# A two-block fp32 network on one core: modulation rows spread over three stages, a two-half norm on VectorE, and recurrence products grouped by the rows they use

## Chip, cores and metric

The kernel runs on one core of a Trainium2 chip. The metric is the device time of one execution in microseconds (us); lower is better. The five engines go by the names of the profile: PE (TensorE matmul, with PEld its weight load), DVE (VectorE), ACT (ScalarE), POOL (GpSimd) and SP (SyncE, which issues the DMAs).

## The reference, cut to what matters

All values are float32, the model width D is 1024. `first_block` maps 256 tokens; `second_block` runs two layers over these tokens and, in its first layer, over 256 context tokens too.

```python
def first_block(x, ...):
    x = x + 0.5 * swiglu(rms_norm(x, ffn1_norm), ffn1_w_in, ffn1_w_out)
    h = rms_norm(x, mix_norm)
    p_rwkv, p_q, p_k, p_v, p_gate = split(h @ w_in)
    y_a = rwkv7_time_mix(p_rwkv, ...)           # recurrence over 256 tokens, 16 heads
    y_b = dilated_attention(p_q, p_k, p_v, ...)
    g_a, g_b = split(sigmoid(p_gate + b_gate))
    x = x + (g_a * (y_a @ w_proj_rwkv) + g_b * (y_b @ w_proj_attn)) @ w_out
    return x + 0.5 * swiglu(rms_norm(x, ffn2_norm), ffn2_w_in, ffn2_w_out)

def rms_norm(x, g):
    return x * rsqrt(mean(x * x, axis=-1) + 1e-6) * g

def step(state, inp):                            # inside rwkv7_time_mix
    sa = einsum('bhvk,bhk->bhv', state, a_t)
    state = state * w_t + sa * b_t + v_t * k_t
    return state, einsum('bhvk,bhk->bhv', state, r_t)
```

In the second block each layer has six modulation rows of 1024 columns per stream, a product of one conditioning vector with `w_ada_2` (1024 by 6144). They scale and shift the norms and gate the residuals: shift, scale and gate of the mixer (columns 0 to 3D), then shift, scale and gate of the ffn (3D to 6D). A mixer runs three branches one after the other, `mlstm`, `diffattn` and `fourier`, each followed by gates and a projection.

## The kernel before

**Matrix products.** Every large product is done in three parts, high times high, low times high and high times low, so each block of weights is needed twice over. `weights` streams them: a 512 KB DMA brings a block `wr` (4 buffers), ACT casts it to `wh` (L202), DVE subtracts to get `wl` (L203), with 3 buffers of each, and PE multiplies (L214 to L216 with tokens on the output rows, L249 to L251 with tokens on the columns). One pass of the loop in `weights` is called a weight iteration here. A scheduler that keeps the data dependences orders the instructions of each engine; on each engine they then run strictly in that order.

**Modulation rows.** `ada(l, c0, c1)` computes columns c0 to c1 in blocks of 512. A block has 8 steps; a step loads 256 KB of `w_ada_2` (`wa`, 4 buffers) and runs two DVE operations, one for each stream, that add a scaled weight block into `aa` (L1134). Then `finish` sums `aa` over the rows with two products on PE (`ada`, L1119; four passes in the trace), copies them on ACT and writes them to memory. `ada` is a generator in `self.fine`; each weight iteration advances it by `self.rate` steps, and what is left when the ffn's own loop is through is run off in one go. The first block's two ffns have 66 weight iterations each, so at rate 0.4 each takes 26 of 48 steps (six blocks, 3D columns) in its loop and, as the code is written, 22 behind it. Layer 1's rows run in layer 0's ffn at rate 1.5.

**Norms.** `rms_row` squares and sums 1024 columns on ACT (L330) and takes the inverse root on POOL: nine small operations on one column, each waiting for the one before it (L331, L286, L290, and L292 and L293 three times). `norm_steps` multiplies x by its gain on DVE (L338) and, when POOL is through, by the root in two halves (L344, or L346 with a shift); PE then transposes the halves (`tr`, L317). There are 22 such norms, two of them the final one, which multiplies at L1602 and L1604 and writes a 1024-column row block with one DMA. `outgoing` runs an output product in two column halves and hands the token tile to the norm when both have been added to X (L459 or L462 and L463).

**The recurrence.** `rwkv_solve` runs for two halves of the heads, eight heads each. In each half it goes over four chunks of 64 tokens. A chunk has, for each head, a product over 128 rows (L818) and, from the second chunk on, a product over 64 rows with the state S (L820), both added up in the same 64 columns of a PSUM tile `pf`. There are two such tiles, one for each parity of the head number; the heads of one parity keep their state in the lower 64 rows, those of the other in the upper 64. ACT copies the outputs O (L824), DVE scales the new state S (L830). Each product shows as two passes in the trace.

## Time and profile before

| what | value |
|---|---|
| median of 3 runs | 2996.85 us (2996.62 to 3001.39) |
| profiled execution, its own time | 3002.16 us |
| its span, first to last instruction | 3000.4 us |
| mean granted TensorE clock | 0.963 of full speed |
| PE / DVE / ACT / POOL busy | 96% / 63% / 40% / 4% |

The span and every row below belong to the one profiled execution. A busy PE is not a PE at its best: its matmuls are pipelined, they run at the clock that was granted at the time (full speed, or half of it), and a switch between kinds of products counts as busy. So a PE that is 96% busy can still lose time in three ways: by idling, at the lower clock, or with products that take longer than they need.

### The profile page before, as it was taken

How to read it: one execution, taken by the hardware profiler on the slowest of the kernel's cores; microseconds unless marked ns; L12 is line 12 of the kernel's file. 1: busy time of each engine (PE TensorE's matmuls, PEld its weight loads, DVE VectorE, ACT ScalarE, POOL GpSimd, SP SyncE). 2: the span in 40 equal slices, each digit the busy share in tenths (PEclk: the TensorE clock that was granted, in tenths of full speed). 3: DMA queues.
4: the chain of work that ended last, by engine and by line, in shares of the span. 5: the costliest groups of instructions: out<-in, count | busy, mean ns of one | idle time of the engine just before them, and what ended most of it. 6: DMA issues, size and time to landing. Idle time of an engine off the chain costs nothing.

```text
span 3000.4 us, 42489 instructions
## 1 busy us (share of the span) xinstructions
PE 2866.2 (96%) x16536; PEld 2436.1 (81%) x16536; DVE 1895.7 (63%) x3228; ACT 1186.0 (40%) x1955; POOL 123.9 (4%) x278
## 2 busy tenths in 40 slices
PE   8988899988998999999999999999999999999998
PEld 7976787777996888987788977877778897799797
DVE  7776958576767455436674266677664555665655
ACT  4434334234443344225442333222344444444443
POOL 1020000002002000000000001000020000000000
PEclk9999979679999999999999999999999999999999
DMA  8766535055674222231233355554442243255564
GB/s 266 222 200 205 169 97 147 32 180 186 211 222 130 67 67 64 75 103 50 64 124 99 88 165 150 159 173 151 155 134 85 85 139 102 78 152 169 168 188 142
DMA packets 298356, 409.59 MB, mean 137 GB/s; under 512 B 31525, under 2 KB 182949, under 8 KB 298154
## 3 DMA queue, kind: packets, MB, share of 16 engines
q1 hardware_dynamic: 298154, 406.87, 44.5%
q8 instruction: 130, 2.13, 0.3%
q14 instruction: 72, 0.59, 0.1%
HBM read 396.98 MB, written 3.24 MB: 133 GB/s over the span
## 4 chain that ended last, share of the span: by engine, by line
PE 80%; DVE 10%; issue 3%; ACT 3%; POOL 2%; DMA 1%; SPq 0%; ACTq 0%; POOLq 0%; DVEq 0%
PE g L215 11%; PE g L216 11%; PE g L214 11%; PE g L249 11%; PE g L251 10%; PE g L250 10%; DVE wl L203 2%; PE dC L1342 2%; PE tr L317 1%; PE I L1318 1%; DVE aa L1134 1%; PE pf L818 1%; ACT dae L1439 1%; PE pf L820 1%; PE f L1509 1%
## 5 line engine op out<-in xcount | busy, mean ns | idle before, releaser
L203 DVE TENSOR_TENSOR wl<-wr,wh 128x1024 fp32r<-128x1024 f32 (+1 forms) x606 | 733.5, 1212 | 630.7 <-ACT wh L202 628.8
L202 ACT CAST wh<-wr 128x1024 fp32r<-128x1024 f32 (+1 forms) x606 | 631.2, 1042 | 1056.2 <-PE g L216 515.6
L215 PE MATMUL g<-wl,xh 128*128 128x512 f32 (+2 forms) x1880 | 733.2, 390 | 13.0 <-DVE wl L203 13.0
L214 PE MATMUL g<-wh,xh 128*128 128x512 f32 (+2 forms) x1880 | 730.0, 391 | 4.4 <-ACT wh L202 2.1
L216 PE MATMUL g<-wh,xl 128*128 128x512 f32 (+2 forms) x1880 | 728.3, 388 | 0.1
L249 PE MATMUL g<-xh,wh 128*128 128x256 f32 (+1 forms) x2352 | 725.9, 309 | 2.2 <-DVE gate L981 1.5
L251 PE MATMUL g<-xh,wl 128*128 128x256 f32 (+1 forms) x2352 | 723.2, 308 | 2.3 <-DVE wl L203 2.3
L250 PE MATMUL g<-xl,wh 128*128 128x256 f32 (+1 forms) x2352 | 722.3, 307 | 0.0
L249 PEld LDWEIGHTS g<-xh,wh 128*128 128x128 f32 x2352 | 452.9, 193 | 33.2 <-issue 7.0
L251 PEld LDWEIGHTS g<-xh,wl 128*128 128x128 f32 x2352 | 453.0, 193 | 25.8 <-DVE wl L203 2.9
L250 PEld LDWEIGHTS g<-xl,wh 128*128 128x128 f32 x2352 | 452.8, 193 | 20.7 <-issue 1.3
L215 PEld LDWEIGHTS g<-wl,xh 128*128 128x128 f32 x1880 | 359.3, 191 | 88.0 <-DVE wl L203 19.5
L214 PEld LDWEIGHTS g<-wh,xh 128*128 128x128 f32 x1880 | 356.6, 190 | 84.1 <-issue 7.5
L216 PEld LDWEIGHTS g<-wh,xl 128*128 128x128 f32 x1880 | 359.4, 191 | 70.5 <-DVE xl L305 1.5
L1134 DVE SCALAR_TENSOR_TENSOR aa<-wa,cond,aa 128x512 f32<-128x512 f32 x336 | 231.9, 745 | 4.8 <-DMA wa<-in_w_ada_dram 4.7
L304 ACT CAST xh<-tr 128x256 fp32r<-128x256 f32 (+1 forms) x114 | 50.4, 463 | 119.8 <-PE tr L317 107.0
L1439 ACT ACTIVATE dae<-sc,dast 128x512 f32<-128x512 f32 (+1 forms) x96 | 58.5, 614 | 42.2 <-DVE dast L1437 37.3
L305 DVE TENSOR_TENSOR xl<-tr,xh 128x256 fp32r<-128x256 f32 (+1 forms) x114 | 57.4, 531 | 18.8 <-ACT xh L304 18.4
L1437 DVE TENSOR_REDUCE dast<-sc 128x1 f32<-128x512 f32 (+1 forms) x96 | 53.8, 597 | 24.2 <-PE sc L1436 23.8
L317 PE MATMUL tr<-ident,hn 128*128 128x128 f32 x160 | 28.5, 315 | 34.1 <-DVE hn L344 17.6
L317 PEld LDWEIGHTS tr<-ident,hn 128*128 128x128 f32 x160 | 22.1, 163 | 43.1 <-DVE hn L344 18.4
L1119 PE MATMUL ada<-aa,one 128*1 128x512 f32 x96 | 30.6, 646 | 27.7 <-DVE aa L1134 27.6
(386 smaller groups left out, 2693.9 us busy)
## 6 DMA issues: line engine op xcount, KB each, us to landing
wr<-in_w_in_dram SPq DMA_DIRECT2D x156, 512.0 KB
wa<-in_w_ada_dram SPq DMA_DIRECT2D x192, 256.0 KB
wr<-in_ffn_w_in_dram SPq DMA_DIRECT2D x88, 512.0 KB
wr<-in_w_ffn_in_dram SPq DMA_DIRECT2D x84, 512.0 KB
wr<-in_w_in_dram SPq DMA_DIRECT2D x156, 256.0 KB
wr<-in_w_ffn_out_dram SPq DMA_DIRECT2D x50, 512.0 KB
wr<-in_ffn_w_out_dram SPq DMA_DIRECT2D x44, 512.0 KB
wr<-in_w_out_dram SPq DMA_DIRECT2D x32, 512.0 KB
```

The costliest lines, as they stand in the source:

```text
L202: nc.scalar.copy(out=wh[:, :kn, :ntot], in_=src)
L203: nc.vector.tensor_tensor(out=wl[:, :kn, :ntot], in0=src, in1=wh[:, :kn, :ntot].bitcast(F32), op=ALU.subtract)
L214: nc.tensor.matmul(o_, xh, wh[:, n0:n1], start=(kc == 0), stop=False)
L215: nc.tensor.matmul(o_, xh, wl[:, n0:n1], start=False, stop=False)
L216: nc.tensor.matmul(o_, xl, wh[:, n0:n1], start=False, stop=(kc == nk - 1))
L249: nc.tensor.matmul(o_, wh[:, fs], xh, start=(kc == 0), stop=False)
L250: nc.tensor.matmul(o_, wh[:, fs], xl, start=False, stop=False)
L251: nc.tensor.matmul(o_, wl[:, fs], xh, start=False, stop=(kc == nk - 1))
L317: self.nc.tensor.transpose(p[:, j * P:(j + 1) * P], src[:, (c + j) * P:(c + j + 1) * P], self.ident)
L1134: nc.vector.scalar_tensor_tensor(out=y, in0=raw, scalar=self.cond[:, k, s:s + 1], in1=acc[s], op0=ALU.mult, op1=ALU.add)
L1342: nc.tensor.matmul(pc[:, 0:257], kw[:, kc * P:(kc + 1) * P], V[t][:, 0:257], start=True, stop=True)
L1439: nc.scalar.activation(out=em, in_=ps[:, 0:n], func=AF.Exp, bias=st[:, m:m + 1], scale=1.0, accum_out=st[:, 2 + m:3 + m])
```

## The change

It has three parts.

- **Modulation rows.** ffn1 now takes columns 0 to 2D (four blocks, 32 steps) at rate 0.6, ffn2 takes 2D to 4D at the same rate, and layer 0's `fourier` branch with its gates takes 4D to 6D at rate 1.4. What is left is run off behind the gates. The gates of the other two branches move into the inner memory pool's scope.
- **Norms.** The sum of squares is split: ACT does columns 0 to 511 as soon as `outgoing` has added them to X (`first_half`), DVE does columns 512 to 1023 with a multiply that accumulates. The inverse root moves from POOL to DVE with a start value that folds in the factor of one half: one operation joins the halves, then come seven more of one column. The final norm multiplies x, root and gain in one operation per half, and each half has a DMA of its own.
- **The recurrence.** A chunk's eight products over 128 rows come first, for both parities into two banks; the eight over 64 rows with the state follow, alternating between lower and upper rows. Copies and states come after them.

```diff
+    def first_half(self, t, x):
+        nc = self.nc
+        a = self.sums[t] = self.s(1, "rn_a", bufs=4)
+        nc.scalar.activation(out=self.h([P, 512], F32, "junk"), in_=x[:, 0:512], func=AF.Square, accum_out=a)
+        nc.vector.tensor_scalar(out=a, in0=a, scalar1=-0.5 / D, scalar2=-0.5e-6, op0=ALU.mult, op1=ALU.add)
+
+    def rms(self, t, x, junk):
...
+        a = self.sums.pop(t)
+        h, y, w = self.s(1, "rn_h"), self.s(1, "rn_y"), self.s(1, "rn_w")
+        nc.vector.scalar_tensor_tensor(out=junk, in0=x[:, 512:D], scalar=1.0, in1=x[:, 512:D], op0=ALU.mult,
+                                       op1=ALU.mult, accum_out=h)
+        nc.vector.tensor_scalar(out=h, in0=h, scalar1=-0.5 / D, scalar2=a[:, 0:1], op0=ALU.mult, op1=ALU.add)
+
+        nc.vector.tensor_scalar(out=y.bitcast(I32), in0=h.bitcast(I32), scalar1=-0.5,
+                                scalar2=float(0x5F3759DF - 0x400000 - 0x40000000), op0=ALU.mult, op1=ALU.add)
+        for _ in range(3):
+            nc.vector.tensor_scalar(out=w, in0=y, scalar1=y[:, 0:1], scalar2=h[:, 0:1], op0=ALU.mult, op1=ALU.mult)
+            nc.vector.tensor_scalar(out=y, in0=w, scalar1=1.5, scalar2=y[:, 0:1], op0=ALU.add, op1=ALU.mult)
+        return y
...
+                banks = [self.t("pf") for _ in range(2)]
+                at = lambda par, pair: banks[par][:, pair * 64:(pair + 1) * 64]
+                for par in range(2):
+                    for pair in range(4):
+                        h = pair * 2 + par
+                        nc.tensor.matmul(at(par, pair), GBf[:, eidx(h), c, 64:192], WV[t][:, c, h, :], start=(pair == 0),
+                                         stop=(ch == 0 and pair == 3))
+                if ch:
+                    for pair in range(4):
+                        for par in range(2):
+                            rows = slice(64 * par, 64 * par + 64)
+                            nc.tensor.matmul(at(par, pair), RG[rows, pair, c].rearrange("p s k -> p (s k)"),
+                                             S[rows, pair, :], start=False, stop=(pair == 3))
...
-            self.fine, self.rate = self.ada(0, 0, 3 * D), 0.4
+            self.fine, self.rate = self.ada(0, 0, 2 * D), 0.6
...
-            self.fine, self.rate = self.ada(0, 3 * D, 6 * D), 0.4
+            self.fine, self.rate = self.ada(0, 2 * D, 4 * D), 0.6
...
+                with self.inner() as self.ip:
+                    if need_ctx:
+                        self.fine, self.rate = self.ada(0, 4 * D, 6 * D), 1.4
+                    self.fourier(xT, W, outs, yT)
+                    gates = {c0: gate(c0) for c0 in range(0, D, n)}
+                    for _ in self.fine:
+                        pass
```

**Place 1: PE at the end of ffn1.** The `g` rows are products (of 512 columns in ffn1, of 288 in the projection behind it), `tr` the norm's transposes, `ada` the products of a modulation block. Before:

```order
L215 MATMUL g<-wl,xh 128x512
L216 MATMUL g<-wh,xl 128x512
L1119 MATMUL ada<-aa,one 1x512 x8
L317 MATMUL tr<-ident,hn 128x128 x12
L214 MATMUL g<-wh,xh 128x288
```

And now:

```order
L215 MATMUL g<-wl,xh 128x512
L216 MATMUL g<-wh,xl 128x512
L309 MATMUL tr<-ident,hn 128x128 x8
L214 MATMUL g<-wh,xh 128x288
L215 MATMUL g<-wl,xh 128x288
L216 MATMUL g<-wh,xl 128x288
```

The eight products of four modulation blocks have left this place, and the first tile's transposes stand directly behind the last product of ffn1; the second tile's eight come 18 products later.

**Place 2: DVE at the same place.** X_69 and X_70 are the two token tiles, `hn` the normed tile, `rn_*` the one-column values of the root, `aa` the modulation sums. Before:

```order
L459 SCALAR_TENSOR_TENSOR X_69<-g,X_69 128x512
L338 TENSOR_TENSOR hn<-X_69,gain 128x1024
L203 TENSOR_TENSOR wl<-wr,wh 128x2x288
L344 TENSOR_SCALAR hn<-hn,rn_y 128x512 x2
L203 TENSOR_TENSOR wl<-wr,wh 128x2x288
L459 SCALAR_TENSOR_TENSOR X_70<-g,X_70 128x512
L1134 SCALAR_TENSOR_TENSOR aa<-wa,cond,ab 128x512
L338 TENSOR_TENSOR hn<-X_70,gain 128x1024
L1134 SCALAR_TENSOR_TENSOR aa<-wa,cond,ab 128x512
L1134 SCALAR_TENSOR_TENSOR aa<-wa,cond,aa 128x512 x14
```

And now:

```order
L481 SCALAR_TENSOR_TENSOR X_69<-g,X_69 128x512
L332 SCALAR_TENSOR_TENSOR hn,rn_h<-X_69 128x512
L334 TENSOR_SCALAR rn_h<-rn_h,rn_a 128x1
L336 TENSOR_SCALAR rn_y<-rn_h 128x1
L339 TENSOR_SCALAR rn_w<-rn_y,rn_h 128x1
L203 TENSOR_TENSOR wl<-wr,wh 128x2x288
L340 TENSOR_SCALAR rn_y<-rn_w,rn_y 128x1
L339 TENSOR_SCALAR rn_w<-rn_y,rn_h 128x1
L340 TENSOR_SCALAR rn_y<-rn_w,rn_y 128x1
L203 TENSOR_TENSOR wl<-wr,wh 128x2x288
```

The modulation sums (32 operations in all behind ffn1) are gone from here; the root's small operations now stand in DVE's row, with the `wl` of the next weights between them.

**Place 3: PE in a recurrence chunk of the first half of the heads.** `pf` with its number is one of the two PSUM tiles, WV and GB belong to the products over 128 rows, S and RG to those over 64 rows. Before, the end of one tile and the start of the other:

```order
L818 MATMUL pf_4023<-WV_2731,GB_2729 128x64
L820 MATMUL pf_4023<-S_3703,RG_3927 128x64
L818 MATMUL pf_4033<-WV_2731,GB_2729 128x64
L820 MATMUL pf_4033<-S_3703,RG_3927 128x64
L818 MATMUL pf_4033<-WV_2731,GB_2729 128x64
```

And now:

```order
L839 MATMUL pf_3933<-WV_2641,GB_2639 128x64 x4
L839 MATMUL pf_3934<-WV_2641,GB_2639 128x64 x4
L845 MATMUL pf_3933<-S_3613,RG_3837 128x64
L845 MATMUL pf_3934<-S_3613,RG_3837 128x64
L845 MATMUL pf_3933<-S_3613,RG_3837 128x64
```

Each row of L818 was followed by one of L820; now the eight over 128 rows stand together, and the eight over 64 rows go to the two tiles in turn.

## Rows read from the trace of the kernel before

**Rows 1.** The page: engines' busy time, and the chain that ended last by engine

```profile
PE 2866.2 (96%) x16536; PEld 2436.1 (81%) x16536; DVE 1895.7 (63%) x3228; ACT 1186.0 (40%) x1955; POOL 123.9 (4%) x278
...
PE 80%; DVE 10%; issue 3%; ACT 3%; POOL 2%; DMA 1%; SPq 0%; ACTq 0%; POOLq 0%; DVEq 0%
```

**Rows 2.** Waits of the span: engine and line, releaser, total us, times, longest us

```profile
PE ada L1119 <- DVE aa L1134: 27.6, 3, 13.2
...
PE tr L317 <- DVE hn L344: 17.6, 3, 11.9
...
PE tr L317 <- DVE hn L346: 16.5, 7, 6.0
...
ACT O L824 <- PE pf L820: 50.7, 12, 5.6
```

**Rows 3.** TensorE's timeline, end of ffn1: start us, us, work, passes, [idle before <-releaser]

```profile
207.53 1.88 PE L1119 MATMUL ada<-aa,one 128*1 128x512 f32 x8
...
222.66 2.53 PE L1119 MATMUL ada<-aa,one 128*1 128x512 f32 x4 [13.25 <-DVE aa L1134]
...
233.66 2.53 PE L1119 MATMUL ada<-aa,one 128*1 128x512 f32 x4 [8.47 <-DVE aa L1134]
...
236.12 1.91 PE L317 MATMUL tr<-ident,hn 128*128 128x128 f32 x12
```

**Rows 4.** VectorE's timeline, same stretch

```profile
203.56 0.69 DVE L459 SCALAR_TENSOR_TENSOR X<-g,X 128x512 f32<-128x512 f32 x1 [1.77 <-PE g L216]
...
213.91 9.36 DVE L1134 SCALAR_TENSOR_TENSOR aa<-wa,cond,aa 128x512 f32<-128x512 f32 x14
```

**Rows 5.** Windows: us, busy PE, PEld, DVE, ACT, POOL (xinstructions), granted clock, DMA share, GB/s

```profile
40.00:200.00 160.00, 160.00 (x1110) 147.78 (x1109) 126.52 (x154) 71.78 (x81) 2.13 (x5) 1.00 0.76 233
330.00:650.00 320.00, 290.26 (x1929) 240.40 (x1930) 226.16 (x537) 111.91 (x237) 3.60 (x7) 0.79 0.39 116
540.00:551.00 11.00, 11.00 (x42) 8.47 (x43) 1.58 (x4) 1.75 (x7) 0.00 (x0) 0.50 0.00 0
1600.00:1750.00 150.00, 150.00 (x904) 133.69 (x903) 48.80 (x64) 47.38 (x65) 0.00 (x0) 1.00 0.30 89
```

**Rows 6.** TensorE's timeline, end of ffn2

```profile
917.24 2.52 PE L1119 MATMUL ada<-aa,one 128*1 128x512 f32 x4 [5.93 <-DVE aa L1134]
...
926.80 0.80 PE L215 MATMUL g<-wl,xh 128*128 128x512 f32 x1 [2.55 <-DVE wl L203]
```

**Rows 7.** Timeline of all engines, the norm at the end of layer 1's mixer

```profile
2787.05 0.69 DVE L463 TENSOR_TENSOR X<-X,rs 128x512 f32<-128x512 f32 x1
...
2793.27 0.75 DVE L346 SCALAR_TENSOR_TENSOR hn<-hn,rn_y,mod 128x512 f32<-128x512 f32 x1 [2.54 <-POOL rn_y L293]
...
2794.08 1.12 PE L317 MATMUL tr<-ident,hn 128*128 128x128 f32 x4 [5.98 <-DVE hn L346]
```

**Rows 8.** VectorE's timeline: two dependent operations of one column

```profile
2275.51 0.16 DVE L1325 SCALAR_TENSOR_TENSOR mlrc<-nd 128x1 f32<-128x1 f32 x1
...
2275.71 0.16 DVE L1327 TENSOR_TENSOR mlrc<-mlrc,mlcf 128x1 f32<-128x1 f32 x1
```

**Rows 9.** TensorE's timeline, recurrence products of several chunks

```profile
392.36 0.43 PE L818 MATMUL pf<-WV,GB 128*128 128x64 f32 x2
...
392.72 0.44 PE L820 MATMUL pf<-S,RG 64*128 64x64 f32 x4
...
530.25 2.10 PE L818 MATMUL pf<-WV,GB 128*128 128x64 f32 x16
...
540.71 0.69 PE L818 MATMUL pf<-WV,GB 128*128 128x64 f32 x2
...
550.58 0.69 PE L768 MATMUL p<-WV,GB 64*64 64x64 f32 x8
```

**Rows 10.** Timeline, the end: last product, last write of y

```profile
2986.85 0.39 PE L216 MATMUL g<-wh,xl 128*128 128x512 f32 x1
...
2996.07 0.76 DVE L1604 TENSOR_SCALAR y<-y,fin_y 128x1024 f32<-128x1024 f32 x1 [3.21 <-POOL fin_y L293]
```

More of the change, by code (lines that the diff above doesn't have):

```diff
@@ L282, in rsqrt @@
         nc = self.nc
[L283 removed]
         y = self.s(n, name + "_y")
         w = self.s(n, name + "_w")
[L286 removed]
+        nc.vector.tensor_scalar(out=y.bitcast(I32), in0=m.bitcast(I32), scalar1=-0.5, scalar2=float(0x5F3759DF),
                                 op0=ALU.mult, op1=ALU.add)
[L288 to L294 removed]
         for _ in range(3):
@@ L324, in to_split @@
                 d += m
-    def rms_row(self, x, name="rn"):
+    def first_half(self, t, x):
         nc = self.nc
-        junk = self.q([P, D], F32, "junk")
-        ss = self.s(1, name + "_s")
-        nc.scalar.activation(out=junk, in_=x, func=AF.Square, accum_out=ss)
-        nc.gpsimd.tensor_scalar(out=ss, in0=ss, scalar1=1.0 / D, scalar2=1e-6, op0=ALU.mult, op1=ALU.add)
-        return self.rsqrt(ss, 1, name)
+        a = self.sums[t] = self.s(1, "rn_a", bufs=4)
[3 more added lines that the diff above has]
+        nc = self.nc
+        if t not in self.sums:
+            self.first_half(t, x)
+        a = self.sums.pop(t)
[9 more added lines that the diff above has]
+        return y
     def norm_steps(self, xT, t, x, gain, shift):
@@ L337, in norm_steps @@
         hn = self.q([P, D], F32, "hn")
-        nc.vector.tensor_tensor(out=hn, in0=x, in1=gain, op=ALU.mult)
-        r = self.rms_row(x)
+        half = lambda v, c: v[:, c:c + 512]
+        if shift is not None:
+            nc.vector.tensor_tensor(out=half(hn, 0), in0=half(x, 0), in1=half(gain, 0), op=ALU.mult)
+        r = self.rms(t, x, half(hn, 512))
+        if shift is not None:
+            nc.vector.tensor_tensor(out=half(hn, 512), in0=half(x, 512), in1=half(gain, 512), op=ALU.mult)
         yield
         for c in range(0, D, 512):
-            v = hn[:, c:c + 512]
+            v = half(hn, c)
             if shift is None:
-                nc.vector.tensor_scalar(out=v, in0=v, scalar1=r[:, 0:1], scalar2=None, op0=ALU.mult)
+                nc.vector.scalar_tensor_tensor(out=v, in0=half(x, c), scalar=r[:, 0:1], in1=half(gain, c), op0=ALU.mult,
+                                               op1=ALU.mult)
             else:
-                nc.vector.scalar_tensor_tensor(out=v, in0=v, scalar=r[:, 0:1], in1=shift[:, c:c + 512], op0=ALU.mult,
+                nc.vector.scalar_tensor_tensor(out=v, in0=v, scalar=r[:, 0:1], in1=half(shift, c), op0=ALU.mult,
                                                op1=ALU.add)
@@ L431, in normed, with outgoing, begin @@
         return xT, done
-    def outgoing(self, xT, nk, W, groups, res, done):
+    def outgoing(self, X, xT, nk, W, groups, res, done):
         whole = lambda g: [(t, 0, 512) for t in g]
+        def begin(g):
+            for t in g:
+                self.first_half(t, X[t])
         if len(groups[0]) > 1:
@@ L440, in outgoing @@
                     res(g, c, self.gemm(xT, nk, W[c], whole(g)))
+                    if c == 0:
+                        begin(g)
                 done(g)
@@ L992, in last_projection @@
                 self.put_split(mT.dst_span(i * per, per, 0, w), M[i].rearrange("p (k t) -> p k t", t=w))
-        self.outgoing(mT, KD, [[(w_out, 0, c * 512, 512)] for c in range(2)], groups, res, nxt())
+        self.outgoing(X, mT, KD, [[(w_out, 0, c * 512, 512)] for c in range(2)], groups, res, nxt())
     def first_block(self, X, nxt):
@@ L1539, in second_layer @@
             yT = SplitT(self, KD, w)
+            gate = lambda c0: [g for c in range(c0, c0 + n, 256) for g in self.gate_chunk(xT, W, U_GATE + b * D + c, w)]
             if fn == "fourier":
-                self.fourier(xT, W, outs, yT)
+                with self.inner() as self.ip:
[5 more added lines that the diff above has]
+                        pass
             else:
@@ L1545, in second_layer @@
                     getattr(self, fn)(xT, W, l, outs, yT)
-            gate = lambda c0: [g for c in range(c0, c0 + n, 256) for g in self.gate_chunk(xT, W, U_GATE + b * D + c, w)]
-            gates = {c0: gate(c0) for c0 in range(0, D, n)}
+                gates = {c0: gate(c0) for c0 in range(0, D, n)}
             if b < 2:
@@ L1601, in done @@
                     y = self.q([P, D], F32, "y")
-                    nc.vector.tensor_tensor(out=y, in0=X[t], in1=g, op=ALU.mult)
-                    r = self.rms_row(X[t], "fin")
-                    nc.vector.tensor_scalar(out=y, in0=y, scalar1=r[:, 0:1], scalar2=None, op0=ALU.mult)
-                    nc.sync.dma_start(out=out[0, t * P:(t + 1) * P, :], in_=y)
+                    r = self.rms(t, X[t], y[:, 512:D])
+                    for c in range(0, D, 512):
+                        nc.vector.scalar_tensor_tensor(out=y[:, c:c + 512], in0=X[t][:, c:c + 512], scalar=r[:, 0:1],
+                                                       in1=g[:, c:c + 512], op0=ALU.mult, op1=ALU.mult)
+                        nc.sync.dma_start(out=out[0, t * P:(t + 1) * P, c:c + 512], in_=y[:, c:c + 512])
             return done
```

32 lines of the change are left out of this document (8 added, 24 removed).

## The prediction

> **What bounds the kernel now.** I read the page first: PE is busy 96% of the span and makes up 80% of the chain that ended last, DVE 10% [rows 1]. So time can only come out of three places: where PE idles, where it runs at the lower clock, and where its products take longer than they must. The view of waits names the idle places that the change touches: PE waits 27.6 us for modulation sums (three times), 17.6 and 16.5 us for normed halves [rows 2]. The windows show the second: from 330 to 650 us, the recurrence and what runs beside it, the granted clock is 0.79 of full speed, where ffn1 has 1.00 [rows 5]. The third is in the recurrence's own rows [rows 9].
>
> **1. Modulation rows at the end of ffn1.** Its last product ends near 207.5 us. Then PE runs products of `ada`, waits 13.25 us for DVE's sums, runs four passes, waits 8.47 us, runs four more, and only at 236.12 us do the norm's transposes start [rows 3]. DVE meanwhile does nothing but such sums, 14 of them in 9.36 us, 0.67 us each [rows 4]. The order of the changed kernel has the transposes right behind the last product (place 1). That opens 236.1 - 207.5 = 28.6 us. Three things come back. The norm was hidden behind the sums and now shows: X is there at 203.56 + 0.69 = 204.25 [rows 4]; squares, eight small operations, two `wl`, the second tile's X and a half of hn stand in DVE's order before the first transpose (place 2), at some 0.7 us for each wide one and 0.2 for a small one about 6 us, so PE waits 2 to 3 us for the first tile, and some 1.2 for the second, whose chain is partly covered by 18 products; I take 4. Two more blocks are finished within the loop, eight passes at the 1.88 us that eight took here [rows 3]. And 12 more sums stand in the loop, 12 x 0.67 = 8 us on DVE, which has 160.0 - 126.5 = 33.5 us free from 40 to 200 us [rows 5]: I take 1, bounds 0 and 4. **28.6 - 4 - 1.9 - 1 = 22**, bounds 18 and 25.
>
> **2. The same at the end of ffn2.** Two waits go, 5.93 and 2.55 us, and with them the four passes between, which took 2.52 us where eight had taken 1.88, so at the lower clock [rows 3, 6]. That is 11.0; products around the waits also ran at that clock, worth some 3. The norm shows again, about 3 to 4 as above. **10**, bounds 6 and 14.
>
> **3. Modulation rows in `fourier`.** The four blocks arrive here: 16 passes at the rate above are 3.8 us of PE, not hidden, since PE is busy 150.0 of 150.0 us there. The 64 sums are 64 x 0.67 = 43 us on DVE, which is busy 48.8 of 150 us, and the loads come on top of a DMA share of 0.30 [rows 5]. What hides them is DVE's spare time of 101 us. Two things could uncover them: up to 13 sums stand in a row in DVE's order here, 8.7 us ahead of one `wl`, which PE has blocks in hand for; and SP's queue issues `wa` and `wr` in turn, so a `wr` can stand behind a `wa` that waits for its buffer. **-4**, bounds -2 and -9, the last for one such run uncovered by half.
>
> **4. Norms.** In the row that shows one whole, X is done at 2787.74, the half of hn starts at 2793.27, 5.5 us later, and PE waits 5.98 us [rows 7]. Now: 0.75 for the squares, eight small operations at 2275.71 - 2275.51 = 0.20 us each [rows 8], 1.6 in all, and a half of x times gain that may come in between, 0.7: 3.1 us, less 2.4 than before. A `wl` in DVE's row adds 1.2 if it comes between. There are ten such waits, 17.6 + 16.5 = 34.1 us [rows 2]. The longest, 11.9, is the start, where x must first land: 2. The one above and the one before ffn2 (about 5.7, what is left of the 17.6 over two waits): 2.2 each. The other six have 16.5 - 6.0 = 10.5 us together, and I take 4 of it, as the `wl` stand in the way. **10**, bounds 4 and 16. The first half's sum on ACT costs nothing: it runs under the second half's products.
>
> **5. The end.** From the last product's end, 2987.2, to the span's end, 3000.4, are 13.2 us of a chain that PE has no part in; the last write of y starts at 2996.07 and takes 0.76 [rows 10]. The root of the last tile gains 2.4 as above, and the first tile's no longer holds up the second's update, while y's halves (0.7 each) stand in DVE's row ahead of the second tile's squares. **3**, bounds 2 and 4.
>
> **6. The recurrence.** Eight products over 128 rows alone take 2.10 us, 0.26 each; between a product over 128 rows and one over 64 the starts are 392.72 - 392.36 = 0.36 us apart. At the lower clock a whole chunk of 16 takes 550.58 - 540.71 = 9.87 us, 0.62 each [rows 9], with the clock at 0.50 [rows 5]. So a change of shape costs about 0.10 at full clock, and at half, where 0.26 would be 0.52, also 0.10. Fourteen of the 16 changes in a chunk go: 1.4 us, and there are six such chunks, 8.4. The row at 392.72 has two products over 64 rows, of opposite halves, done within 0.44 us: 0.22 each, and less than 0.26 if their end is a tail that the next covers. Such pairs are now the rule; eight products at 0.18 to 0.22 instead of 0.26 give 0.3 to 0.6 per chunk, twice that at the lower clock: 2 to 6 in all. ACT's wait for these products (50.7 us) [rows 2] gets no shorter: both parities now end together, so one of the copies starts later, and some of the gain may go there. **12**, bounds 4 and 22.
>
> The Trainium skill ("TensorEngine Tiling (Array Packing)", Key Properties) says that a change of tiling mode drains the engine, and that different tiles run in parallel. By the second sentence eight products over 64 rows would take the time of four, an estimate of half their time by that page; the row at 392.72 allows it for one pair and shows no more. What this would give is the second rival.
>
> **The sum.** 22 + 10 - 4 + 10 + 3 + 12 = 53 us. The profiled execution took 3002.2, so 2949; the median lies 5.3 lower (2996.85), and all runs of before lie within 5 us. **2943.5 us.** All lower bounds add up to 18 + 6 - 9 + 4 + 2 + 4 = 25 (2972), all upper ones to 25 + 14 - 2 + 16 + 4 + 22 = 79 (2918).
>
> **Rivals.**
> - *The root on DVE waits where POOL did not.* DVE runs in order, and each norm's chain now stands between `wl` and sums. If two `wl` come into each chain, the norms give 3 instead of 10 and the ends of the ffns 4 less: 42 us, 2955. For: the order shows `wl` in the chain (place 2). Against: it is POOL that PE waits for at the dear ones [rows 7].
> - *The two halves run side by side throughout.* Then the eight products over 64 rows take 4 x 0.26 at full clock instead of 8 x 0.26, 1.0 less per chunk, about 1.5 at the mean clock of 0.79: 6 x 1.5 = 9 less what is counted for it, 5 more: 2938.
> - *The recurrence's gain is absorbed.* PE is busy 290 of 320 us there [rows 5], so it waits 30 us already, for DVE and ACT; a shorter run of products then only waits longer: 8 to 10 us of the 12 are lost, 2953.
> - *The clock in 330 to 650 us falls further.* The mechanism: the lower clock comes after PE has waited (four passes took 2.53 us behind a 13.25 us wait, eight had taken 1.88 ahead of it [rows 3]); if the same work leaves more gaps between shorter bursts, more of it runs at half speed. PE's 290 us of work at 0.79 become 290 x 0.79 / c. At c = 0.70 that is 37 us more: 2980. It ends above 2996.85 when the loss exceeds 53 us, below c = 0.67; at c = 0.60, 92 us more, 3035. For: the stage sits between both levels already, and a chunk ran at 0.50 throughout [rows 5] with PE busy all the time. Against: nothing in the change adds a wait there. The other way is as open: c = 0.85 gives back 20 us, 2923.
> - *It doesn't do what it says.* The order shows that it does at all three places; only the gains could be missing.
>
> **How the numbers follow.** Forecast as summed (2932 to 2951): 0.42. Root in DVE's row: 0.18. Absorbed recurrence: 0.12. Side by side: 0.12. Clock better: 0.05. Clock worse: 0.08, of which half within the gain (2960 to 2990), a quarter no change, a quarter slower. Something that none of these names: 0.03. The range from 2915 to 2973 takes in all bounds of the unknown costs and the cases up to the worse clock. About 0.2% (6 us) is what a measurement of this kernel can tell from no change: faster by more 0.93, within 0.03, slower 0.04.
>
> **What would show it.** Right: no wait for `aa` in the list of PE's waits, the transposes at the end of ffn1 within 5 us of its last product; `fourier` without a gap at PE; chunks of 6 to 8 us where the clock is half; DVE's busy time up by the small operations, POOL near nothing; waits of PE for hn down by a third or more. Wrong: PE waiting for `wl` in ffn1 or `fourier` (step 1 or 3), waits for hn as long as before with DVE as releaser (step 4), chunks as long as before or a granted clock below 0.79 from 300 to 620 us (step 6).

## The result, and the profile after

The changed kernel takes 2926.82 us (median of 4 runs, 2922.90 to 2931.51), the kernel before 2996.73 us on the same chip (2995.43 to 3001.39). The ratio is 0.9765 with a 95% interval of 0.9743 to 0.9787: it is faster by 70 us. The forecast was 2943.5, a gain of 53. The sign, the range and the mechanism of four of the six steps held; the recurrence gave three times what was forecast, and the norms a quarter. The forecast's own central stretch, 2932 to 2951, was missed: the time is below it.

The profiled execution of the changed kernel took 2930.70 us with a span of 2928.9, at a mean granted clock of 0.978 against 0.963. The page, the lines that answer to [rows 1]:

```profile
PE 2823.6 (96%) x16536; PEld 2407.4 (82%) x16536; DVE 1933.8 (66%) x3478; ACT 1176.4 (40%) x1955; POOL 22.4 (1%) x81
...
PE 80%; DVE 13%; ACT 3%; DMA 2%; issue 2%; SPq 0%; DVEq 0%; ACTq 0%
```

PE is as busy in share as before, but 43 us less in all; DVE has 38 us more, POOL 101 us less. The waits (engine and line, releaser, total us, times, longest us) that answer to [rows 2]:

```profile
ACT O L852 <- PE pf L845: 22.6, 7, 4.7
...
PE g L215 <- DVE wl L203: 21.0, 11, 4.7
...
PE tr L309 <- DVE hn L357: 17.5, 3, 10.0
...
PE tr L309 <- DVE hn L360: 6.8, 1, 6.8
```

PE's waits for modulation sums (27.6 us) are gone from this view, and ACT's wait for the recurrence's products has fallen from 50.7 to 22.6 us. The waits for normed halves fell only from 34.1 to 24.3 us, by 29% where the forecast's sign was a third or more, and waits for `wl` rose from 13.0 (in the same view of before) to 21.0.

Both kernels run the same 12,696 products `g`, in the same order but for some 2% of the places, where neighbours have changed places; so the start of the n-th one in both traces tells where time was won. The table gives what each stretch of before (by its own times) became shorter (negative) or longer, in us of the span; the other columns are the experiments below.

| stretch of before, us | changed | e1_rec | e2_ada | e3_norm | e4_noalt | e5_half0 | e6_pool2 | e7_halfpool | e8_mix | e9_rate1 |
|---|---|---|---|---|---|---|---|---|---|---|
| start, to 25 | -2.7 | -0.5 | -0.4 | -2.5 | -2.7 | -0.6 | -1.8 | -2.0 | -2.2 | -2.1 |
| ffn1, to 190 | +2.4 | +0.1 | +2.6 | -0.1 | +2.0 | 0.0 | +1.5 | +1.5 | +2.2 | +1.7 |
| end of ffn1, to 260 | -23.3 | -0.2 | -18.0 | -1.7 | -22.6 | -0.6 | -23.1 | -23.4 | -21.8 | -23.2 |
| to 350 | -0.9 | -0.9 | -1.4 | -1.7 | -1.4 | -1.4 | -1.8 | -1.8 | -1.3 | -0.3 |
| recurrence, first half, to 505 | -16.9 | -16.9 | -4.3 | -1.0 | -18.8 | -18.1 | -19.0 | -19.1 | -15.1 | -16.9 |
| second half and what follows, to 690 | -20.7 | -20.6 | 0.0 | -0.6 | -19.5 | +0.1 | -23.1 | -23.1 | -23.1 | -20.4 |
| norm before ffn2, to 765 | -2.8 | +0.6 | +2.0 | -3.7 | -2.7 | +0.1 | +0.3 | +0.9 | -2.8 | -2.6 |
| ffn2, to 890 | +2.3 | 0.0 | +2.3 | 0.0 | +2.3 | 0.0 | +2.3 | +2.3 | +2.3 | +2.3 |
| end of ffn2, to 1010 | -16.2 | +0.4 | -14.0 | +7.4 | -16.7 | +1.4 | -12.0 | -13.4 | -16.3 | -16.5 |
| fourier, 1565 to 1760 | +7.6 | -0.9 | +4.8 | -0.4 | +3.9 | -0.6 | +4.3 | +4.4 | +4.7 | +4.1 |
| layer 0's ffn norm, to 1870 | -1.2 | 0.0 | +1.3 | -3.2 | -1.3 | -0.2 | +1.1 | +0.8 | -1.3 | -1.6 |
| layer 1's mixer norm, 2150 to 2280 | +3.6 | -2.8 | -1.7 | +4.4 | +4.4 | -2.9 | -1.6 | +1.8 | -1.8 | +4.7 |
| layer 1's ffn norm, 2770 to 2860 | +0.4 | 0.0 | -0.1 | -0.1 | -0.2 | +0.7 | -0.2 | +1.6 | 0.0 | +2.7 |
| the end, from 2980 | -2.8 | 0.0 | +0.1 | -2.7 | -2.8 | 0.0 | -2.6 | -2.8 | -2.7 | -2.7 |
| whole span | -71.5 | -41.5 | -26.9 | -6.4 | -75.5 | -22.1 | -75.8 | -71.5 | -79.4 | -71.0 |

Each column is one profiled execution, laid against one of before that was 5 us longer than before's median; so the columns add up to 2 to 11 us more than the medians differ by, and differences of 2 to 4 us in a stretch can be chance: e1_rec and e5_half0 have layer 1's norm as before and still stand 2.8 and 2.9 us below before's one execution there, and e2_ada has the recurrence as before and stands 4.3 us below in its first half. Stretches left out changed by less than 0.7 us.

The end of ffn1, to be laid beside [rows 3] (start us, us, work, passes, [idle before <-releaser]):

```profile
206.92 0.39 PE L216 MATMUL g<-wh,xl 128*128 128x512 f32 x1
209.73 1.44 PE L309 MATMUL tr<-ident,hn 128*128 128x128 f32 x8 [2.42 <-DVE hn L357]
211.07 0.40 PE L214 MATMUL g<-wh,xh 128*128 128x288 f32 x1
```

The last product ends at 207.31, the transposes start 2.42 us later, the next weights' products run from 211.07. Before, the transposes started at 236.12.

The recurrence, to be laid beside [rows 9]: a chunk at half clock, then one at full clock.

```profile
499.44 3.67 PE L839 MATMUL pf<-WV,GB 128*128 128x64 f32 x16
503.04 1.97 PE L845 MATMUL pf<-S,RG 64*128 64x64 f32 x16
504.94 1.33 PE L790 MATMUL p<-WV,GB 64*64 64x64 f32 x20
```

```profile
524.33 1.89 PE L839 MATMUL pf<-WV,GB 128*128 128x64 f32 x16
526.15 1.11 PE L845 MATMUL pf<-S,RG 64*128 64x64 f32 x16
527.19 0.55 PE L937 MATMUL tr<-ident,dsc 128*128 128x128 f32 x3
```

From 540.71 to 550.58 the first of these took 9.87 us before; now it is 499.44 to 504.94, 5.50 us, at the same clock of 0.50 (second row below). At full clock a chunk is 2.86 us. Within it, eight products over 128 rows take 1.82 us (0.23 each) and eight over 64 rows 1.04 us, 0.13 each.

The windows (columns as in [rows 5]) of the recurrence's stage, of that chunk and of the fourier branch:

```profile
303.00:588.00 285.00, 253.74 (x1937) 212.80 (x1936) 229.04 (x539) 114.04 (x239) 3.60 (x7) 0.86 0.44 134
499.00:505.00 6.00, 6.00 (x36) 5.33 (x34) 1.17 (x3) 0.99 (x4) 0.00 (x0) 0.50 0.00 0
1523.00:1679.00 156.00, 155.69 (x925) 135.09 (x924) 77.17 (x107) 52.23 (x74) 1.61 (x4) 1.00 0.38 122
```

The stage that had a granted clock of 0.79 has 0.86, and needs 254 us of PE where it needed 290. In the fourier branch PE still has no gap to speak of (155.7 of 156.0 us busy), with DVE up from 48.8 of 150 to 77.2 of 156 us.

### The profile page after: what moved, and what is told of

Read it like the earlier page. It is cut to its first block, busy times and chain, and to the rows that moved or that the text cites. A ratio compares the mean times of both kernels' runs of the same rounds, so it can differ in the third digit from the quotient of the medians.

```text
span 2928.9 us, 42526 instructions
## 1 busy us (share of the span) xinstructions
PE 2823.6 (96%) x16536; PEld 2407.4 (82%) x16536; DVE 1933.8 (66%) x3478; ACT 1176.4 (40%) x1955; POOL 22.4 (1%) x81
## 4 chain that ended last, share of the span: by engine, by line
PE 80%; DVE 13%; ACT 3%; DMA 2%; issue 2%; SPq 0%; DVEq 0%; ACTq 0%
PE g L215 12%; PE g L216 12%; PE g L214 11%; PE g L249 10%; PE g L251 10%; PE g L250 10%; DVE wl L203 3%; PE dC L1370 2%; PE tr L309 1%; PE I L1346 1%; DVE aa L1162 1%; ACT dae L1467 1%; ACT wh L202 1%; PE ada L1147 1%; PE f L1537 1%
## 5 line engine op out<-in xcount | busy, mean ns | idle before, releaser
L250 PEld LDWEIGHTS g<-xl,wh 128*128 128x128 f32 x2352 | 450.8, 192 | 20.9 <-issue 1.3
L1370 PE MATMUL dC<-vo,kw 128*128 128x257 f32 x192 | 50.3, 394 | 0.0
L1162 DVE SCALAR_TENSOR_TENSOR aa<-wa,cond,ab 128x512 f32<-128x512 f32 x48 | 34.9, 746 | 20.1 <-PE ada L1147 16.7
```

Source lines behind the costliest of these rows:

```text
L250: nc.tensor.matmul(o_, wh[:, fs], xl, start=False, stop=False)
L1162: nc.vector.scalar_tensor_tensor(out=y, in0=raw, scalar=self.cond[:, k, s:s + 1], in1=acc[s], op0=ALU.mult, op1=ALU.add)
L1370: nc.tensor.matmul(pc[:, 0:257], kw[:, kc * P:(kc + 1) * P], V[t][:, 0:257], start=True, stop=True)
```

## The experiments

In every run the time of before was taken on the same chip: 2996.42 us for the first four, 2998.80 for e5 to e7, 2997.05 for e8 and e9. Times are compared as ratios or as differences to these.

### One part at a time: e1_rec, e2_ada, e3_norm

**e1_rec** is the kernel before with the third part of the change alone.

```diff
-                        nc.tensor.matmul(o_, GBf[:, eidx(h), c, 64:192], WV[t][:, c, h, :], start=True, stop=(ch == 0))
-                        if ch:
-                            nc.tensor.matmul(o_, RG[rows, pair, c].rearrange("p s k -> p (s k)"), S[rows, pair, :],
...
+                        nc.tensor.matmul(at(par, pair), GBf[:, eidx(h), c, 64:192], WV[t][:, c, h, :], start=(pair == 0),
```

> The kernel before with the recurrence's products regrouped and nothing else. In the trace of the changed kernel the stretch from the first attention products to the end of the recurrence (250 to 650 us of before) came out 38.7 us shorter, where the forecast had 12; its chunks themselves are some 27 us shorter, the rest is a higher granted clock. Theory A, the regrouping alone does it (shorter products, and a clock that falls less often because of them): the whole stretch is 36 to 40 us shorter here too, time about 2958 to 2961. Theory B, the clock outside the chunks rose because of the other two parts (an earlier start, fewer waits ahead of the stage): only 27 us come, time about 2970. The forecast's price: 12 us, 2985.

Measured: 2961.30 us, ratio 0.9884 (0.9869 to 0.9899), 35 us less than before. The table has 38.4 us between 260 and 690, as many as in the changed kernel, and next to nothing elsewhere but in one norm. So theory A holds: the regrouping alone gives the whole gain of the stage, 35 us by the medians and 38.4 by the table, and the forecast's 12 us were far too few.

**e2_ada** moves the modulation rows and changes nothing else.

```diff
-            self.fine, self.rate = self.ada(0, 0, 3 * D), 0.4
+            self.fine, self.rate = self.ada(0, 0, 2 * D), 0.6
...
-            self.fine, self.rate = self.ada(0, 3 * D, 6 * D), 0.4
+            self.fine, self.rate = self.ada(0, 2 * D, 4 * D), 0.6
...
+                        self.fine, self.rate = self.ada(0, 4 * D, 6 * D), 1.4
```

> The kernel before with the modulation rows moved and nothing else. Theory, by the stretches of the changed kernel's trace: the end of ffn1 gives 20 to 23, the end of ffn2 some 14, the fourier branch takes 7 to 8 back: 27 to 29 us, time about 2968 to 2970. Rival: part of that is the faster norm, which here still hangs on the root on GpSimd and shows once the sums no longer hide it (about 5.5 us from X to the normed half instead of 3 to 4, at both ends): 22 to 24 us, 2973 to 2975.

Measured: 2974.60 us, ratio 0.9927 (0.9912 to 0.9941), 22 us less: the rival's size. The end of ffn1 gives 18.0 instead of 23.3 and the end of ffn2 14.0 instead of 16.2. The waits for normed halves show why; they grew from 17.6 and 16.5 us [rows 2]:

```profile
PE tr L317 <- DVE hn L344: 20.5, 5, 11.9
PE tr L317 <- DVE hn L346: 19.2, 8, 6.0
```

With the sums gone, PE waits there for the norm, whose root is still on GpSimd.

**e3_norm** changes the norms and nothing else (the first two pieces of the diff, and the calls of `outgoing` that hand X on).

```diff
-        nc.scalar.activation(out=junk, in_=x, func=AF.Square, accum_out=ss)
-        nc.gpsimd.tensor_scalar(out=ss, in0=ss, scalar1=1.0 / D, scalar2=1e-6, op0=ALU.mult, op1=ALU.add)
-        return self.rsqrt(ss, 1, name)
+    def rms(self, t, x, junk):
```

> The kernel before with the norms changed and nothing else. Theory, by the stretches of the changed kernel: 2.7 at the start, 2.8 in front of ffn2, 1.2 in layer 0, minus 3.7 and minus 0.4 in layer 1, 2.8 at the end, nothing at the ffn ends where the modulation sums still hide the norm: 5 us, time about 2991 to 2993. Forecast's price: 10 for the norms and 3 for the end, 2984. Rival: behind the modulation sums, which stand in VectorE's row, the small operations come later still: no gain or a loss, 2997 or more.

Measured: 2993.64 us (10 runs), ratio 0.9992 (0.9982 to 1.0001): no difference that the interval allows to state. The table gives 2.5 at the start, 3.7 in front of ffn2, 3.2 in layer 0 and 2.7 at the end, as in the changed kernel or better, and takes 4.4 at layer 1's mixer norm and 7.4 at the end of ffn2. The waits of the whole span:

```profile
PE ada L1141 <- DVE aa L1156: 29.7, 3, 11.0
...
PE g L215 <- DVE wl L203: 27.2, 12, 5.9
```

29.7 us for sums instead of 27.6, and 27.2 us for `wl` instead of 13.0. At the end of ffn2 PE's two waits, 5.93 us for sums and 2.55 us for `wl` [rows 6], became 9.95 and 5.89, which is the 7.4 us: the norm's operations stand in the same row of DVE as the sums, and what PE needs comes later. The three parts alone give 35 + 22 + 3 = 60 us, together 70: the norm on DVE is worth more where the sums have left, and the sums' leaving is worth more where the norm is short.

### The recurrence: e4_noalt and e5_half0

**e4_noalt** keeps the two groups of eight, but runs the 64-row products tile by tile, so that four neighbours use the same half of the rows.

```diff
-                    for pair in range(4):
-                        for par in range(2):
+                    for par in range(2):
+                        for pair in range(4):
```

> The changed kernel with the eight 64-row products of a chunk in the order of the tiles (four of one row half, then four of the other) instead of alternating. Theory A, alternating halves run side by side: the eight products take about 1.9 us instead of 1.04 in a chunk at full clock, five chunks have that form, 4 to 6 us in all, time about 2931 to 2933, and the trace shows the passes 0.11 us apart instead of 0.065. Theory B, only the fewer changes of shape count: no difference, 2927.

Measured: 2932.01 us, theory A's time, ratio 0.9781 (0.9766 to 0.9796), against 0.9765 for the changed kernel: 5 us more by the medians, but the intervals overlap, and of the two profiled executions this one is the shorter, by 3.7 us in the fourier branch and 2 in the first half's stretch. So the chunk itself has to decide; the one that is followed by `tr` at L911, at full clock:

```profile
390.07 2.00 PE L839 MATMUL pf<-WV,GB 128*128 128x64 f32 x16
392.00 1.60 PE L845 MATMUL pf<-S,RG 64*128 64x64 f32 x16
393.54 0.66 PE L911 MATMUL tr<-ident,dsq 128*128 128x128 f32 x4
```

Eight products over 64 rows take 1.54 us (392.00 to 393.54), where the alternating order takes 1.04. In this form the alternation is worth 0.5 us a chunk at full clock, and 0.9 at half (6.41 us against 5.50). Theory A had 1.9 us for this order, not 1.54; the first passes of the group tell why. Two cuts of the same row, up to the second pass and up to the fourth, and two of the changed kernel's, up to the fourth and up to the eighth:

```profile
392.00 0.43 PE L845 MATMUL pf<-S,RG 64*128 64x64 f32 x2
392.00 0.66 PE L845 MATMUL pf<-S,RG 64*128 64x64 f32 x4
```

```profile
526.15 0.44 PE L845 MATMUL pf<-S,RG 64*128 64x64 f32 x4
526.15 0.66 PE L845 MATMUL pf<-S,RG 64*128 64x64 f32 x8
```

In e4_noalt one more product on the same half adds 0.23 us; in the changed kernel two more, on opposite halves, add 0.22. So theory A holds for the mechanism, and while it lasts two products take the time of one. Eight products one behind the other at 0.22 would be 1.8 us, more than the 1.54 measured: where the two groups of four meet, some of e4_noalt's own products run side by side too, and the 0.5 us is less than the whole worth of it.

The rest of the chunk's gain is the fewer changes of shape. Of one shape a product takes 0.22 to 0.23 us, over 128 rows (eight in 1.82) as over 64; in turn they stand 0.36 apart [rows 9], so a change costs 0.14. Sixteen in turn are 5.8 us, the chunk is now 2.86: of these 2.9 us the 14 changes that went are 2.0, and the halves side by side the other 0.9 or so. Before, every second neighbour also added into the columns that the product ahead of it had just written; that is no rival for the 0.14, since the spacing is the same 0.36 from such a product to the next, which goes to other columns (424.08, 424.44, 424.81 and 425.17 us in before).

The Trainium skill ("TensorEngine Tiling (Array Packing)", Key Properties) has both: a change of tiling mode drains the engine, and different tiles work in parallel. The traces agree with the second: two products on opposite halves add 0.22 us, as one alone does. They show a price at each change, 0.14 us, as the first would have it; that it is a drain, no run here shows.

**e5_half0** is the kernel before, with the products regrouped in the first half of the heads only.

```diff
+                if hh == 0:
+                    banks = [self.t("pf") for _ in range(2)]
...
+                else:
+                    pf = []
```

> The kernel before, with the recurrence's products regrouped in the first half of the heads only. Regrouping both halves shortened the stretch up to the second half (before's 350 to 530 us) by some 17 us and the stretch of the second half (530 to 620) by some 20, with chunks of the first half at full clock where before they had 0.68 to 0.88, and about 22 us fewer of half clock in the second. Theory A, products that alternate between 128 and 64 rows bring the lower clock with them: the first half gains its 17 us here too, the second half keeps the old chunks (7.4 to 9.9 us) at the old clock of 0.50 to 0.75, and time is about 2979. Theory B, the clock of a half hangs on what comes before it (start of the stage, waits for VectorE), not on its own products: the second half's clock rises too although its products are the old ones, and its chunks take 5.8 us: about 2970.

Measured: 2979.15 us, ratio 0.9940 (0.9926 to 0.9953), 20 us less. The windows of both halves: before, this kernel, and e1_rec, where both halves are regrouped.

```profile
330.00:515.00 185.00, 173.59 (x1174) 145.21 (x1174) 142.32 (x339) 71.70 (x127) 1.55 (x3) 0.89 0.46 133
515.00:650.00 135.00, 116.67 (x761) 95.19 (x759) 83.84 (x199) 40.21 (x110) 2.05 (x4) 0.65 0.29 92
```

```profile
327.00:494.00 167.00, 154.67 (x1169) 130.53 (x1168) 143.13 (x339) 72.02 (x128) 1.55 (x3) 0.96 0.51 148
494.00:629.00 135.00, 116.59 (x757) 94.97 (x758) 83.74 (x199) 40.06 (x111) 2.04 (x4) 0.65 0.28 91
```

```profile
329.00:497.00 168.00, 156.81 (x1184) 132.49 (x1185) 142.63 (x339) 71.74 (x127) 1.56 (x3) 0.95 0.50 148
497.00:611.00 114.00, 95.54 (x751) 79.55 (x748) 83.47 (x199) 40.24 (x110) 2.05 (x4) 0.72 0.33 108
```

The first half rose from 0.89 to 0.96 and is 18 us shorter; the second has the old clock, 0.65, the old length, 135 us, and the old chunks:

```profile
520.00 0.69 PE L839 MATMUL pf<-WV,GB 128*128 128x64 f32 x2
520.62 0.69 PE L841 MATMUL pf<-S,RG 64*128 64x64 f32 x2
...
529.87 1.44 PE L768 MATMUL p<-WV,GB 64*64 64x64 f32 x22
```

16 products, 0.62 us apart at half clock, 9.87 us as in [rows 9]. In e1_rec the second half has 0.72 and is 21 us shorter. So theory A holds for the rise: the clock rose in the half whose own products were regrouped, and only there. PE's waits have no part in it. Between the products `g` that stand at 350 and 505 us of before, PE idles 6.5 to 7.0 us in all eleven kernels; the granted clock there is 0.89 to 0.92 in the three with the old products (before, e2_ada, e3_norm), and 0.95 to 0.99 in the eight with the new.

What came before a chunk is not without effect, though. The second half's first chunk with a state ran at 0.50 in every kernel, regrouped or not. In the changed kernel the clock was low already in the 7 us ahead of it, in which PE was busy for 3.01:

```profile
492.00:499.00 7.00, 3.01 (x12) 2.42 (x12) 4.45 (x26) 1.68 (x4) 0.00 (x0) 0.51 0.00 0
```

### The norms: e6_pool2, e7_halfpool, e8_mix

**e6_pool2** is the changed kernel with the second block's norms as before.

```diff
+        if shift is not None:
+            nc.vector.tensor_tensor(out=hn, in0=x, in1=gain, op=ALU.mult)
+            r = self.rms_row(x, "rp")
```

> The changed kernel, with the four norms of the second block that have a shift computed as before: the whole sum on ScalarE, the root on GpSimd. In the changed kernel these stretches gave 1.2 us in layer 0, lost 3.7 and 0.4 in layer 1. Theory A, the root's small operations stand in VectorE's row among the weights' subtractions and hold these up: 2 to 4 us faster than the changed kernel, about 2923 to 2925, the waits of TensorE for wl at the layer 1 norm (2.99 and 4.68 us) gone, waits of 2.2 to 2.4 us for hn in their place. Theory B, the loss comes from the shift of times alone: no difference, 2927.

Measured: 2926.62 us, ratio 0.9764 (0.9751 to 0.9778): the same as the changed kernel. That is theory B's number, but not its reason. Layer 1's mixer norm is 5.2 us better (-1.6 against +3.6) as theory A had it, and the stretch before ffn2 3.1, the end of ffn2 4.2 and layer 0's ffn norm 2.3 us worse. The waits moved from `wl` to normed halves:

```profile
PE tr L309 <- DVE hn L379: 18.8, 8, 6.0
...
PE g L215 <- DVE wl L203: 10.3, 7, 4.3
```

21.0 us for `wl` became 10.3, and 6.8 us for halves with a shift became 18.8.

**e7_halfpool** keeps the halved sum and takes only the joining and the root of those norms to GpSimd.

```diff
+            r = self.rms(t, x, half(hn, 512), None if shift is None else nc.gpsimd)
```

> The changed kernel, with the sum still in two halves (ScalarE and VectorE), but the joining of the halves and the root of the four norms with a shift on GpSimd. Theory A (small operations in VectorE's row are what costs): the squares of the second half take 0.7 us on VectorE and GpSimd's chain about 3, so X to hn is about 4 us against 5.5 before and 6.3 in the changed kernel at the norm that waits 6.8 us; 3 to 6 us faster than the changed kernel, 2921 to 2924. Theory B: the squares on VectorE hold up the weights as much as the small operations did: 2926 to 2928.

Measured: 2934.70 us, ratio 0.9793 (0.9780 to 0.9806): above the changed kernel by the medians, but the intervals overlap, and neither theory's time. Theory A's price for the chain was right, at the norm that waits longest:

```profile
2716.66 0.69 DVE L486 TENSOR_TENSOR X<-X,rs 128x512 f32<-128x512 f32 x1
...
2721.52 0.75 DVE L361 SCALAR_TENSOR_TENSOR hn<-hn,rn_y,mod 128x512 f32<-128x512 f32 x1 [2.24 <-POOL rn_y L341]
...
2722.33 1.11 PE L309 MATMUL tr<-ident,hn 128*128 128x128 f32 x4 [4.62 <-DVE hn L361]
...
2726.10 1.69 POOL L335 TENSOR_SCALAR rn_h<-rn_h,rn_a 128x1 f32<-128x1 f32 x1 [4.61 <-DVE hn L333]
...
2731.74 0.65 PE L309 MATMUL tr<-ident,hn 128*128 128x128 f32 x4 [1.91 <-DVE hn L361]
```

From X at 2717.35 to the half at 2721.52 are 4.2 us, and PE waits 4.62 instead of 6.77. But the second tile takes this back: its squares come late in VectorE's row, GpSimd has nothing to do for 4.61 us until they are done, and PE waits 1.91 us for this tile's half, for which it doesn't wait in the changed kernel. The expectation counted one tile, and the norm has two. The stretch as a whole is +1.6 in the table against +0.4, which is within chance, and the profiled execution's span is the changed kernel's (2928.9 us): where the medians' 8 us arise stays open.

**e8_mix** puts back only the norms of layer 1, where the table shows a loss, and keeps the others.

```diff
+                self.early = False
...
+        if shift is not None and not self.early:
+            nc.vector.tensor_tensor(out=hn, in0=x, in1=gain, op=ALU.mult)
+            r = self.rms_row(x, "rp")
```

> The changed kernel with only layer 1's six norms (mixer and ffn) computed as before, whole sum on ScalarE and root on GpSimd; layer 0's norms stay as changed. With all second-block norms put back, the trace showed 5.2 us less at layer 1's mixer norm and 0.6 us less at its ffn norm, and some 4.6 us more at the norm behind ffn2 and 1.9 more at layer 0's ffn norm. Theory A, the split pays where VectorE's row is short and costs where the subtractions for the next weights stand in it: both gains are kept, 4 to 6 us faster than the changed kernel, 2921 to 2923. Theory B, these differences are the scheduler's accidents and come out otherwise in any new order: 2925 to 2929.

Measured: 2919.36 us (5 runs, 2914.72 to 2929.54), ratio 0.9749 (0.9727 to 0.9771). The table keeps both gains, -1.8 at layer 1's mixer norm and -16.3 and -1.3 at layer 0's, which is theory A; waits for `wl` and for halves with a shift are both short:

```profile
PE g L215 <- DVE wl L203: 13.2, 9, 5.0
...
PE tr L309 <- DVE hn L383: 10.6, 3, 6.0
```

By the medians it is the fastest kernel of the study, 7 us below the changed one; the intervals of the two ratios overlap, so the step from the changed kernel to this one is shown by the stretch and not by the times. There the table is clear: at layer 1's mixer norm the four kernels with the whole new norm stand at +3.6 to +4.7, the five that have the old one there at -1.6 to -2.9, and before itself at 0.

### The fourier branch: e9_rate1

```diff
-                        self.fine, self.rate = self.ada(0, 4 * D, 6 * D), 1.4
+                        self.fine, self.rate = self.ada(0, 4 * D, 6 * D), 1.0
```

> The changed kernel with the modulation rows in the fourier branch at rate 1.0 instead of 1.4. At 1.4 the trace shows the branch 7.6 us longer: 4.6 us of products for the sums of four blocks, 2.5 us in which TensorE waits for a gate that stands behind sums in VectorE's row ahead of the branch, 0.6 of a late wl. Theory A, the runs of sums in VectorE's row are what the rest of the loss comes from: thinner, it falls from 3 to about 1 us, 2 us faster, about 2925. Theory B, eight steps remain for the end and there hold up the gates' weights: 1 to 3 us slower, 2928 to 2930. The forecast's bound for the whole step was 9 us.

Measured: 2928.72 us, ratio 0.9775 (0.9756 to 0.9795): no difference. The branch takes 4.1 us more than before where the changed kernel's profiled execution shows 7.6, but e4_noalt, e6_pool2 and e8_mix, which have the rate of 1.4, show 3.9 to 4.7. So the rate does nothing that shows, and neither theory is needed. What the 7.6 had beyond that was one wait of 2.5 us in one execution, and its row shows the step that can go wrong (VectorE, just ahead of the branch, where the scheduler has drawn the first sums forward):

```profile
1494.67 4.93 DVE L1162 SCALAR_TENSOR_TENSOR aa<-wa,cond,aa 128x512 f32<-128x512 f32 x7 [2.81 <-DMA wa<-in_w_ada_dram]
...
1500.65 3.40 DVE L1162 SCALAR_TENSOR_TENSOR aa<-wa,cond,aa 128x512 f32<-128x512 f32 x5
...
1505.10 1.28 DVE L1009 SCALAR_TENSOR_TENSOR gate<-gate,g 128x512 f32<-128x512 f32 x2
```

The sums wait 2.81 us for `wa` to land, seven and five of them and two `wl` follow, and only at 1505.10 does the gate come for which PE waits.

## Why the prediction was right, step by step

- **Modulation rows at the end of ffn1 (22, bounds 18 and 25): right.** 23.3 less 2.4 in the loop is 20.9. The first tile's wait came out at 2.42 us (forecast 2 to 3). The 12 more sums in the loop cost no more than 0.5 us, which is what the loop's 2.4 us have above the 1.9 that I had for the products of two more blocks.
- **End of ffn2 (10, bounds 6 and 14): too small.** 16.2 less 2.3 in the loop is 13.9, just within the bound. I charged the norm 3 to 4 us here; the table of e2_ada against the changed kernel says that the new norm gives 2 of these back.
- **Modulation rows in fourier (-4, bounds -2 and -9): right.** 3.9 to 4.8 in six kernels, 7.6 in one execution with the wait named above, still within the bounds. It is the products of the sums, 16 passes, that are paid; DVE's sums and the loads are hidden.
- **Norms (10, bounds 4 and 16): wrong, 2.7, outside the bounds.** 2.7 at the start and 2.8 in front of ffn2 are as forecast (2 and 2.2), 1.2 in layer 0; layer 1 lost 3.6 and 0.4. The step that failed is the 2.2 at the dear norm and the 4 for "the other six": the first rival, the root on DVE waiting where POOL did not, decided both, and its 3 us for the norms came true; the 4 us that it took from the ends of the ffns did not. At the norm of [rows 7]:

```profile
2718.59 0.69 DVE L485 TENSOR_TENSOR X<-X,rs 128x512 f32<-128x512 f32 x1
...
2722.11 1.22 DVE L203 TENSOR_TENSOR wl<-wr,wh 128x1024 fp32r<-128x1024 f32 x1
...
2723.36 1.22 DVE L203 TENSOR_TENSOR wl<-wr,wh 128x1024 fp32r<-128x1024 f32 x1
...
2725.61 1.42 DVE L360 SCALAR_TENSOR_TENSOR hn<-hn,rn_y,mod 128x512 f32<-128x512 f32 x2
...
2726.42 1.97 PE L309 MATMUL tr<-ident,hn 128*128 128x128 f32 x8 [6.77 <-DVE hn L360]
```

X is done at 2719.28 and the half starts at 2725.61, 6.3 us, where before it was 5.5. The chain has the small operations that I counted, at some 0.28 us each rather than 0.20 (the last four take 1.11 us, from 2724.50 to 2725.61), but it also holds two `wl` of 1.2 us each, the second tile's update of X, and a half of x times gain. I had priced one `wl` as a possibility; DVE's order put two in. PE waits 6.77 us, 5.98 before.
- **The end (3): right, 2.8.** From PE's last product to the last write of y:

```profile
2918.12 0.39 PE L216 MATMUL g<-wh,xl 128*128 128x512 f32 x1
...
2924.34 1.41 DVE L1638 SCALAR_TENSOR_TENSOR y<-X,rn_y,fg 128x512 f32<-128x512 f32 x2
```

The span ends 10.4 us behind the last product's end at 2918.51, not 13.2.
- **The recurrence (12, bounds 4 and 22): mis-sized, 38.5, outside the bounds.** Two things were wrong. First, the price of a product: I took 0.26 us for one that follows its own shape, from the 2.10 us of eight at 530.25 [rows 9], and so had 0.10 left for the change. That row begins at the lower clock (granted 0.50 up to 530.5) and counts the end of the last product too. A product of one shape takes 0.22 (e4_noalt) and a change 0.14: 2.0 us a chunk for the changes instead of 1.4, and 0.9 for the halves side by side instead of 0.3 to 0.6; 2.9 in all at full clock, some 17 us for six chunks. Second, and larger, the clock: I priced the chunks at the clock that they had, and named a better clock only as a chance of 1 in 20. Before, the six chunks had granted clocks of 0.50 to 0.88; regrouped, all but the one shown above have 1.00. The rest of the 38.5, about 21 us, is what is left for the clock, in these chunks and in the products around them. That is a remainder, not a measurement. For it speak that PE's idle time there did not change (e5_half0), and that the lower level was granted for some 130 us between 350 and 690 us of before and for some 75 in the same stretch now.

That the time still lies in the range is in part luck. The range was wide because it took in a better and a worse clock; the recurrence gave 26 us more than its term, the norms 7 less, and some 21 us of it, the higher clock, are a case that I had given 0.05.

Of the signs, the absence of waits for `aa`, the transposes 2.42 us behind ffn1's last product, a `fourier` with hardly a gap and a clock of 0.86 where below 0.79 would have been wrong came as named. Two did not: the chunk at half clock took 5.50 us, below the "6 to 8", and the waits for hn fell by 29%, less than a third. The rival of side-by-side halves came true in its mechanism, with 0.9 us a chunk where I had 1.0. The rival that the gain would be absorbed did not; ACT's wait for the products, of which I had said that it would get no shorter, halved.

## What to carry to other kernels

Group small matrix products by the rows that they use before anything else is tuned around them, and let neighbours use opposite halves of the rows; count a change of shape at its measured price, and look at the granted clock of the stretch as well, which here rose with the regrouping. Work taken out of a waiting engine's way (here sums at the end of a loop) pays what its wait was, less what the next one in line then shows: move the chain behind it too, and count both together. A chain of small dependent operations belongs on the engine whose queue is short at that place; on an engine that runs in order, price it with the long operations that the order puts in between, for each tile, not with its own lengths.

## What the runs showed of the hardware that was not expected

- The granted clock fell while PE was never idle by the records. Before, PE has no gap from 401 to 434 us; the clock is at its upper level (2.4 GHz) up to 428 and then at its lower one (1.2 GHz). The fall lies in the middle of a chunk that runs from 424.08 to 431.16, in which products over 128 and over 64 rows alternate:

```profile
401.00:428.00 27.00, 27.00 (x223) 20.75 (x222) 16.98 (x23) 13.80 (x24) 0.00 (x0) 1.00 0.35 98
428.00:434.00 6.00, 6.00 (x26) 5.34 (x26) 2.00 (x7) 1.32 (x2) 0.00 (x0) 0.51 0.49 175
```

  With the same products in two groups this chunk has 1.00 in the changed kernel, and e5_half0 ties the rise to the half that is regrouped. What in the alternation lowers the clock (the changes themselves, or the lower rate of work) was not tried and stays open.
- A change between products over 128 and over 64 rows, of 64 columns each, costs 0.14 us at full clock, 0.36 less 0.22; at half it is 0.19, as the eight at 499.44 take 3.60 us with one change behind them, 0.43 each, where products in turn stand 0.62 apart. A product itself takes 0.22 at full clock, over 64 rows as over 128.
- Two 64-row products on opposite halves add 0.22 us together, as much as one alone; eight take 1.04 us alternating, 1.54 in e4_noalt's order.
